# The end of an eight-core encoder kernel: weights of the last group kept resident, its tiles run one after another, early output stores moved

## Chip, cores, metric

One Trainium2 chip, all eight NeuronCores, one program on each. A core computes 2048 of 16384 tokens with a halo of 60 on each side; nothing is exchanged between cores. The metric is the device time of one launch, that of the slowest core, in microseconds (us).

The executions fall into a fast state and a slow one, in which the cores of one die (0 to 3, 4 to 7) or of both show a lower granted TensorE clock. A profile is of one execution; it lists span and granted clock of each core.

## The reference, cut

```python
for l in range(DEPTH):          # 4 layers, D_MODEL 1024, D_FF 2816
    x = layer_norm(ALPHA * x + 0.5 * swiglu_ffn(x, ffn1...), ln1_g, ln1_b)
    x = layer_norm(ALPHA * x + hybrid_mixer(x, ...), ln2_g, ln2_b)
    x = layer_norm(ALPHA * x + 0.5 * swiglu_ffn(x, ffn2...), ln3_g, ln3_b)
# swiglu_ffn: (silu(x @ w_gate) * (x @ w_up)) @ w_down
```

## The kernel before

The activations lie transposed in on-chip memory: 1024 features as 8 chunks of 128 partitions, tokens along the free dimension, as fp32 (`xs`) and as bf16 (`xb`). The tokens of a core are cut into two halves (`s` = 0, 1) and each half into three tiles. While the FFN of one half runs on TensorE, the mixer or the layer norms of the other half run on the other engines. A small list scheduler in Python places every instruction, so each engine executes a fixed order. In the names of the profiles, `bank` is an accumulator of TensorE, `PEld` its weight loads, `sg` and `HF` the gate after silu and the product with up, and `HM`, `Y`, `ringM` memory that belongs to the mixer and is lent to the norms and, in the change, to the weights.

```python
def tiles_of(rng):              # three nearly equal tiles; 352, 352, 352 for the last half
    ...

class Ring:                     # weight blocks of 128 x 1024, five slots, loaded by the POOL queue
    def release(self, k):
        self.load(k + self.ns)  # a freed slot loads the block five places ahead
```

An FFN goes through its 22 blocks of the inner dimension in three groups of 8, 7 and 7. In each group every block is used for all three tiles before the next:

```python
for gi, (j0, nj) in enumerate(GROUPS):      # (0, 8), (8, 7), (15, 7)
    for jj in range(nj):
        kg, ku = ringF.take(), ringF.take()
        for ti, (c0, n) in enumerate(tiles):
            # gate: 8 matmuls, up: 8 matmuls; then silu on ACT, product on DVE -> HF
            ...
        ringF.release(kg); ringF.release(ku)
    for dc in range(NKC):                   # 8 output chunks
        k = ringF.take()
        for ti, (c0, n) in enumerate(tiles):
            # nj matmuls; then xs[dc] += bank on DVE ("evacuation")
            ...
        ringF.release(k)
spawn_ln(s, li, which)                      # three layer norm tiles
```

A layer norm tile sums over the 1024 features with matmuls against ones. VectorE adds pairs of chunks first, so that only four small matmuls are needed. Then come ten VectorE operations for mean and 1/sqrt(var), four "normalise passes" over 4 chunks each, and the affine on ScalarE:

```python
e1 = tt(t1, XS3(0, 2, c0, n), XS3(2, 2, c0, n), ALU.add)   # DVE: pairs of chunks
...                                                        # ACT: squares, DVE: their sums
mm_part(banks[0][1], n, [(ones_v, row_of(t1, c, n)) for c in range(2)], True, True)
pe_ev = mm_part(banks[1][1], n, [(ones_v, row_of(q1, c, n)) for c in range(2)], True, True)
ev = yield from stats(rst, nmr, nm, t_, banks[0], banks[1], n, inv, pr - 0.5)
for h in range(2):
    x = XS3(4 * h, 4, c0, n)
    e1 = tt(x, x, rst, ALU.mult, ...)                      # DVE, 4 x n elements
    zev.append(tt(x, x, nmr, ALU.add, ...))                # DVE, 4 x n elements
...
if final:                                                  # the last norm of the last layer
    dma("sp", dram(out3[:, :, o0:o0 + n]), XS3(0, NKC, c0, n), f"st{s}{ti}", ...)
```

Of the kernel before, what the change touches and what calls it, by code (L numbers as in the profile page):

```python
# [10 lines left out]
ALU = mybir.AluOpType  # L11

P = 128
# [47 lines left out]
def tiles_of(rng):  # L61
    lo, hi = rng
    units = (hi - lo) // 4
    base, rem = divmod(units, 3)
    out = []
    for i in range(3):
        n = 4 * (base + (1 if i < rem else 0))
        out.append((lo, n))
        lo += n
    return out  # L70
# [273 lines left out]
def build():  # L344
# [254 lines left out]
            self.load(k + self.ns)  # L599

    F_ORDER = [(s, li, f) for li in range(nl) for f in range(2) for s in range(2)]
    planF, planM = [], []
    for s, li, f in F_ORDER:
        base = li * 2 + f
        for j0, nj in GROUPS:
            for jj in range(nj):
                row = wgud[base * NJ + j0 + jj]
                planF.append((row[:, 0:1024], 1024))
                planF.append((row[:, 1024:2048], 1024))
            for dc in range(NKC):  # L610
                planF.append((wdd[base * NKC + dc][:, j0 * P:(j0 + nj) * P], nj * P))
# [69 lines left out]
        yield Need("dve", [e1], prio=prio)  # L681
        return tt(nmr, nm, rst, ALU.mult)

    def ln_tile(s, li, which, ti, c0, n, final):
        yp = y_prom(s, li, which)[ti]
        goff, boff = V_LN[which]
        inv = 1.0 / D
        pr = 0.1 * ti
        yield Need("dve", [yp], [(lnp, 1)], prio=pr, cond=lambda: st["m"] == 0)
        st["ln"] += 1  # L690
        u = lnp.get()
        pair = lambda k: lnu_bf(u[1], k, n, 1)
        t1, t2, q1, q2 = pair(0), pair(1), pair(2), pair(3)
        e1 = tt(t1, XS3(0, 2, c0, n), XS3(2, 2, c0, n), ALU.add)
        e2 = None
        for k in range(4):
            yield Need("act", [yp, e2], prio=pr - 0.3)
            e = act(q2 if k else q1, XS3(2 * k, 2, c0, n), AF.Square)
            if k == 0:
                yield Need("dve", [yp], prio=pr - 0.3)  # L700
                tt(t2, XS3(4, 2, c0, n), XS3(6, 2, c0, n), ALU.add)
            else:
                yield Need("dve", [e], prio=pr - 0.3)
                e2 = tt(q1, q1, q2, ALU.add, rate=2.0)
            if k == 1:
                yield Need("dve", [e1], prio=pr - 0.3)
                e1 = tt(t1, t1, t2, ALU.add, rate=2.0)
        yield Need("pe", [e1, e2], [(bankB, 2)], prio=-1e9)
        banks = (bankB.get(), bankB.get())
        mm_part(banks[0][1], n, [(ones_v, row_of(t1, c, n)) for c in range(2)], True, True)  # L710
        pe_ev = mm_part(banks[1][1], n, [(ones_v, row_of(q1, c, n)) for c in range(2)], True, True)
        yield Need("act", [pe_ev], prio=pr - 0.5)
        t_, nm, rst, nmr = [lnu_f32(u[1], k, n) for k in range(4)]
        ev = yield from stats(rst, nmr, nm, t_, banks[0], banks[1], n, inv, pr - 0.5)
        zev = []
        for h in range(2):
            x = XS3(4 * h, 4, c0, n)
            yield Need("dve", [ev], prio=pr)
            e1 = tt(x, x, rst, ALU.mult, bap=bcast(rst, 4, n))
            yield Need("dve", [e1], prio=pr)  # L720
            zev.append(tt(x, x, nmr, ALU.add, bap=bcast(nmr, 4, n)))
        lnp.put(u, zev[1])
        st["ln"] -= 1
        e1 = None
        if not final:
            for c in range(NKC):
                yield Need("act", [zev[c // 4]], prio=pr)
                e1 = act(XB(c, c0, n), XS(c, c0, n), AF.Identity, scale=vcol(goff + c, li), bias=vcol(boff + c, li))
            xb_prom(s, li, which)[ti].add(e1)
        if which == 0 or final:  # L730
            for c in range(NKC):
                yield Need("act", [zev[c // 4]], prio=pr if final else pr + 2)
                if final:
                    act(XS(c, c0, n), XS(c, c0, n), AF.Identity, scale=vcol(goff + c, li), bias=vcol(boff + c, li))
                else:
                    act(XS(c, c0, n), XS(c, c0, n), AF.Identity, scale=agcol(li, c), bias=agcol(li, 8 + c))
        if final:
            o0 = c0 - HALO
            dma("sp", dram(out3[:, :, o0:o0 + n]), XS3(0, NKC, c0, n), f"st{s}{ti}", n * 4 * NKC * P / 1e6)

    def spawn_ln(s, li, which):
        rng = in_range(s, li) if which == 0 else out_range(s, li)
# [13 lines left out]
    def ffn(s, li, f):  # L756
        rng = in_range(s, li) if f == 0 else out_range(s, li)
        tiles = tiles_of(rng)
        lo = rng[0]
        if f == 1:  # L760
            xp, which = xb_prom(s, li, 1), 2
        elif li > 0:
            xp, which = xb_prom(s, li - 1, 2), 0
        else:
            xp, which = x0P[s], 0
        yp = y_prom(s, li, which)
        if f == 0:
            ag = (lambda c: agcol(li - 1, 32 + c)) if li > 0 else (lambda c: ALPHA)
            ab = (lambda c: agcol(li - 1, 40 + c)) if li > 0 else None
        else:  # L770
            ag = lambda c: agcol(li, 16 + c)
            ab = lambda c: agcol(li, 24 + c)
        for gi, (j0, nj) in enumerate(GROUPS):
            slots = [(hs["n"] + i) % NHS for i in range(nj)]
            hs["n"] += nj
            hP = [PromiseN(nj) for _ in range(3)]
            for jj in range(nj):
                kg, ku = ringF.take(), ringF.take()
                for ti, (c0, n) in enumerate(tiles):
                    yield Need("pe", [xp[ti], ringF.ev[kg], ringF.ev[ku]], [(bankF, 2)], prio=f_prio)  # L780
                    g, u = bankF.get(), bankF.get()
                    ge = mm([(g[1], n, [(ringF.w(kg, k), XB(k, c0, n)) for k in range(NKC)])])
                    ue = mm([(u[1], n, [(ringF.w(ku, k), XB(k, c0, n)) for k in range(NKC)])])
                    st["vtF"] += 2 * NKC * n / 2400.0

                    def silu(ti=ti, c0=c0, n=n, g=g, u=u, ge=ge, ue=ue, hslot=slots[jj], hP=hP):
                        b = sgp.get()
                        sg = view2("sg", sg_t, 4, b[1], NMAX, 0, n)
                        ae = act(sg, bank(g[1], n), AF.Silu)
                        bankF.put(g, ae)  # L790

                        def hmul():
                            de = stt(HF(hslot, c0 - lo, n), sg, 0.5, bank(u[1], n), ALU.mult, ALU.mult)
                            bankF.put(u, de)
                            sgp.put(b, de)
                            hP[ti].add(de)
                        S.task(Need("dve", [ae, ue], prio=-1), hmul)
                    S.task(Need("act", [ge], [(sgp, 1)], prio=-1), silu)
                ringF.release(kg)
                ringF.release(ku)  # L800
                if late and gi == 0 and jj > 1:
                    late.pop(0)(ue)
            for dc in range(NKC):
                k = ringF.take()
                for ti, (c0, n) in enumerate(tiles):
                    yield Need("pe", [hP[ti], ringF.ev[k]], [(bankF, 1)], prio=f_prio)
                    b = bankF.get()
                    me = mm([(b[1], n, [(ringF.w(k, i), HF(slots[i], c0 - lo, n)) for i in range(nj)])])
                    st["vtF"] += nj * n / 2400.0

                    def evac(dc=dc, ti=ti, c0=c0, n=n, b=b, gi=gi):
                        x, ps = XS(dc, c0, n), bank(b[1], n)
                        if gi == 0:
                            de = stt(x, x, ag(dc), ps, ALU.mult, ALU.add)
                        elif gi == 1 and ab is not None:
                            de = stt(x, ps, ab(dc), x, ALU.add, ALU.add)
                        else:
                            de = tt(x, x, ps, ALU.add)
                        bankF.put(b, de)
                        if gi == len(GROUPS) - 1:  # L820
                            yp[ti].add(de)
                    S.task(Need("dve", [me], prio=-1), evac)
                ringF.release(k)
        spawn_ln(s, li, which)

    def f_chain():
        for s, li, f in F_ORDER:
# [385 lines left out]
    with ExitStack() as stack:  # L1213
# [22 lines left out]
        def _(e):  # L1236
            p.replay("sp", e, sems)
            for s in range(2):
                for ti in range(3):
                    e.wait_ge(sems[f"st{s}{ti}"], 16)  # L1240
    build.prog = p
    return nc

# [122 lines left out]
```

## Time and profile before

| | kernel before |
|---|---|
| median of all 15 executions, fast and slow | 4927.84 us |
| mean of the 7 fast ones | 4771.3 us |
| profiled execution (fast) | 4776.15 us, cores 4764.0 to 4774.6 |
| TensorE busy | 98% |
| wait of TensorE on a weight load in the last FFN, by core | 4.4 to 11.9 us |
| from the end of the last weight matmul to the end of the span | 57.2 to 60.3 us |

The prediction shows the lines that carry this. Columns: names, issuing queue, count, kB, us from issue to landing.

```profile
out<-xs SPq DMA_DIRECT2D x1, 1408.0 KB, 5.7
```

```profile
out<-xs SPq DMA_DIRECT2D x1, 1408.0 KB, 8.6
```

It is the same last store of the same program. It took 5.6 to 6.2 us on six cores, 8.5 and 8.6 on cores 4 and 5. In the middle of their stores these two moved 200 to 240 GB/s each, the other six some 350 to 380.

### The profile page before, as it was taken

The numbers are of one execution on the slowest core, as the hardware profiler recorded it, in microseconds if no ns is written. First come the engines' busy times: TensorE is split into PE (matmuls) and PEld (weight loads), VectorE is DVE, ScalarE is ACT, GpSimd is POOL, SyncE is SP. The second block draws the span as 40 slices with busy tenths as digits, with TensorE's granted clock in tenths as the row PEclk, the third lists the DMA queues.
The fourth block names the chain that finished last, engine by engine and source line by source line (L and its number), as shares of the span: only waits on it lengthen the run. The fifth ranks groups of instructions, "written<-read, shape, count | busy, mean of one in ns | idle before, by whom it ended". The sixth has DMA issues, their size and how long they took to land.

```text
span 4774.6 us, 80409 instructions; the slowest of 8 cores (4764.0 to 4774.6 us)
## 1 busy us (share of the span) xinstructions
PE 4666.3 (98%) x31440; PEld 3053.1 (64%) x31440; DVE 2760.5 (58%) x4632; ACT 1486.7 (31%) x2751; POOL 808.5 (17%) x1524
## 2 busy tenths in 40 slices
PE   7999999999999999999999999999999999999995
PEld 4666666666666666666666666666666666666563
DVE  2265775762627577566363757757445556756635
ACT  1143343231314334333131433433212242443312
POOL 1112112111111211211111121221111121121110
PEclk9999999999999999999999999999999999999997
DMA  8557558556565755755555665665556575575663
GB/s 146 69 69 107 73 70 110 73 73 73 73 71 72 105 75 80 102 74 73 74 74 74 87 95 74 95 88 75 74 73 77 75 101 85 72 107 72 95 79 67
DMA packets 232106, 394.03 MB, mean 83 GB/s; under 512 B 27456, under 2 KB 85312, under 8 KB 231744
## 3 DMA queue, kind: packets, MB, share of 16 engines
q0 software_dynamic: 204544, 364.77, 59.2%
q1 hardware_dynamic: 27200, 24.12, 2.2%
q8 instruction: 265, 4.34, 0.4%
q14 instruction: 97, 0.79, 0.1%
HBM read 725.32 MB, written 8.39 MB: 154 GB/s over the span
## 4 chain that ended last, share of the span: by engine, by line
PE 93%; DVE 4%; DMA 1%; issue 1%; ACT 1%; SPq 0%; ACTq 0%; POOLq 0%; DVEq 0%
PE bank L492 92%; DVE HM L529 2%; PE bank L500 1%; DVE xs L529 1%; DMA ringF<-wgu 1%; DVE HM L535 1%; DMA xs<-xin 1%; ACT HM L522 0%; DVE HF L535 0%; DVE Y L535 0%; DVE HM L542 0%; ACT xb L522 0%; ACT xs L522 0%; SPq L555 0%; DVE tiny L529 0%
## 5 line engine op out<-in xcount | busy, mean ns | idle before, releaser
L492 PE MATMUL bank<-xb,ringF 128*128 128x352 bf16 (+7 forms) x16896 | 2554.2, 312 | 38.3 <-ACT xb L522 24.8
L492 PEld LDWEIGHTS bank<-xb,ringF 128*128 128x128 bf16 x16896 | 1639.5, 97 | 922.1 <-issue 44.0
L492 PE MATMUL bank<-HF,ringF 128*128 128x352 bf16 (+8 forms) x8448 | 1277.1, 312 | 0.0
L522 ACT ACTIVATE sg<-bank 128x352 f32<-128x352 f32 (+8 forms) x1200 | 555.8, 463 | 2188.3 <-PE bank L492 2170.5
L535 DVE SCALAR_TENSOR_TENSOR HF<-sg,bank 128x352 bf16<-128x352 f32 (+8 forms) x1056 | 547.3, 519 | 1030.0 <-PE bank L492 988.4
L492 PEld LDWEIGHTS bank<-HF,ringF 128*128 128x128 bf16 x8448 | 822.5, 97 | 434.6
L555 POOL DMA_DIRECT2D ringF<-wgu x704 | 371.9, 528 | 2187.0 <-PE bank L492 2148.6
L529 DVE TENSOR_TENSOR xs<-xs,bank 128x352 f32<-128x352 f32 (+8 forms) x624 | 324.1, 521 | 323.0 <-PE bank L492 323.0
L492 PE MATMUL bank<-xb,ringM 128*128 128x352 bf16 (+8 forms) x3264 | 501.0, 313 | 0.2 <-ACT xb L522 0.2
L529 DVE TENSOR_TENSOR xs<-xs,HM 128x1408 f32<-128x1408 f32 (+8 forms) x288 | 464.8, 1617 | 1.2
L529 DVE TENSOR_TENSOR HM<-HM 128x352 f32<-128x352 f32 (+23 forms) x640 | 405.2, 649 | 39.7 <-ACT HM L522 31.2
L492 PEld LDWEIGHTS bank<-xb,ringM 128*128 128x128 bf16 x3264 | 316.8, 97 | 173.6 <-issue 0.9
L522 ACT ACTIVATE HM<-xs 128x704 bf16<-128x704 f32 (+8 forms) x288 | 221.3, 784 | 576.5 <-DVE xs L529 330.5
L555 POOL DMA_DIRECT2D ringF<-wd x384 | 203.5, 530 | 988.1 <-PE bank L492 972.3
L522 ACT ACTIVATE xb<-xs,vecs 128x352 bf16<-128x352 f32 (+7 forms) x528 | 330.3, 673 | 50.0 <-DVE xs L529 49.5
L535 DVE SCALAR_TENSOR_TENSOR xs<-xs,agb,bank 128x352 f32<-128x352 f32 (+3 forms) x336 | 191.7, 578 | 215.3 <-PE bank L492 215.0
L492 PE MATMUL bank<-Y,ringM 128*128 128x352 bf16 (+5 forms) x1584 | 238.5, 311 | 7.1 <-DVE tiny L529 4.4
L535 DVE SCALAR_TENSOR_TENSOR xs<-bank,agb,xs 128x352 f32<-128x352 f32 (+3 forms) x336 | 192.6, 580 | 77.8 <-PE bank L492 77.8
L492 PEld LDWEIGHTS bank<-Y,ringM 128*128 128x128 bf16 x1584 | 154.5, 98 | 88.3 <-issue 9.3
L535 DVE SCALAR_TENSOR_TENSOR HM<-HM 128x352 f32<-128x352 f32 (+12 forms) x320 | 164.9, 515 | 7.2
L535 DVE SCALAR_TENSOR_TENSOR HM<-sg,bank 128x352 bf16<-128x352 f32 (+6 forms) x72 | 125.0, 1737 | 51.0 <-PE bank L492 51.0
L555 POOL DMA_DIRECT2D ringM<-win x136 | 73.3, 540 | 355.1 <-PE bank L492 353.3
(46 smaller groups left out, 1397.0 us busy)
## 6 DMA issues: line engine op xcount, KB each, us to landing
ringF<-wgu POOLq DMA_DIRECT2D x704, 256.0 KB, 5.8
ringF<-wd POOLq DMA_DIRECT2D x256, 224.0 KB, 4.4
ringM<-win POOLq DMA_DIRECT2D x136, 256.0 KB, 4.8
ringF<-wd POOLq DMA_DIRECT2D x128, 256.0 KB, 4.9
ringM<-wcn POOLq DMA_DIRECT2D x96, 288.0 KB, 6.4
ringM<-wout POOLq DMA_DIRECT2D x64, 256.0 KB, 4.5
xs<-xin SPq DMA_DIRECT2D x6, 744.0 KB, 21.2
out<-xs SPq DMA_DIRECT2D x3, 1408.0 KB, 8.6
```

The lines of the kernel that those rows point to most:

```text
L492: ins = e.matmul(banks_t[b][:, :n], l.ap, r.ap, start=(i == 0), stop=(i == len(prs) - 1))
L500: ins = e.matmul(banks_t[b][:, :n], l.ap, r.ap, start=start and i == 0, stop=stop and i == len(prs) - 1)
L522: return p.emit("act", lambda e: e.activation(out=out.ap, in_=in_.ap, func=func, bias=bi, scale=sc), R, [out], dur=k + size_of(out) * 0.00 ...
L529: return dve(lambda e: e.tensor_tensor(out=out.ap, in0=a.ap, in1=bap if bap is not None else b.ap, op=op), out, [a, b], rate)
L535: return dve(lambda e: e.scalar_tensor_tensor(out=out.ap, in0=a.ap, scalar=s_, in1=bap if bap is not None else b.ap, op0=op0, op1=op1), ou ...
L555: return p.emit(eng, lambda e: e.dma_start(out=out.ap, in_=in_.ap), R, W, dur=0.55 if eng == "pool" else 0.6, dma=sem, mbytes=mbytes, afte ...
```

## The change

The intent: two norms of the last FFN shall run under TensorE's work instead of after it, the last tile shall have a short norm, and the stores of the first half shall leave when no weight load is under way. To run tile by tile, all 22 blocks of the last group must be resident; they go into memory that the mixer no longer needs.

```diff
 def tiles_of(rng):
     ...
+        if rng == out_range(1, DEPTH - 1):
+            n = (372, 372, 312)[i]

+    def short_sums(u, yp, c0, n):             # the last tile only
+        for h in range(2):
+            e1 = copy(cast, XS3(4 * h, 4, c0, n))          # DVE: bf16
+            e2 = act(sq, XS3(4 * h, 4, c0, n), AF.Square)  # ACT
+            mm_part(... ones x 4 rows of cast ...); mm_part(... ones x 4 rows of sq ...)

+        if short:                             # affine: six chunks on ACT, two on DVE
+            for h in range(2):
+                ...
+                dma("sp", dram(out3[:, 4 * h:4 * h + 4, o0:o0 + n]), ...)   # store in halves
+            if s == 0:
+                late_st.append(put)           # the first half's stores wait
+            else:
+                put()

+            if (s, li, f, gi) == LAST:
+                spawn_ln(s, li, which)
+                for ti in range(3):
+                    for t, jj in [(ti, j) for j in range(ti > 0, nj)] + [(ti + 1, 0)] * (ti < 2):
+                        ue = yield from gate_up(lastW[2 * jj], lastW[2 * jj + 1], ...)
+                        while late_st:
+                            late_st.pop(0)([ue])
+                    for dc in range(NKC):
+                        yield from down(lastW[2 * nj + dc], ...)
+                return
     ...
+                if (s, li, f) == LAST[:3]:
+                    load_last(1)              # one early block per gate/up step of groups 1, 2
     ...
+                if (s, li, f) == LAST[:3] and gi == 1:
+                    load_last(1)              # and per down chunk of group 2
```

## The prediction

> **What bounds the kernel now.** I began with the page's busy times and its slices: is this one long stage or several?
>
> ```profile
> PE 4666.3 (98%) x31440; PEld 3053.1 (64%) x31440; DVE 2760.5 (58%) x4632; ACT 1486.7 (31%) x2751; POOL 808.5 (17%) x1524
> PE   7999999999999999999999999999999999999995
> PEclk9999999999999999999999999999999999999997
> ```
>
> TensorE is busy for 98% of 4774.6 us. Only the first and last slices (119 us each) have holes. The change doesn't touch the first, and it removes no matmul: what it can win are holes of TensorE. Next, the list of waits from 4300 us until the last large matmul, and the timeline at the place where it points:
>
> ```profile
> PE bank L492 <- DMA ringF<-wgu: 11.9, 1, 11.9
> ```
>
> ```profile
> 4493.07 39.36 SPq L555 DMA_DIRECT2D out<-xs  x3
> ...
> 4502.52 6.13 PE L492 MATMUL bank<-xb,ringF 128*128 128x352 bf16 x40
> 4520.53 14.72 PE L492 MATMUL bank<-xb,ringF 128*128 128x352 bf16 x88 [11.87 <-DMA ringF<-wgu]
> ```
>
> One wait of 11.9 us. It lies inside the three output stores of the first half of the sequence, issued from 4493 us on while the last FFN streams its weights. Reading the same wait on all eight cores, the longest single wait on this load is 7.2, 4.4, 7.9, 9.0, 11.9, 11.9, 8.6 and 6.4 us, against spans of 4770.0, 4764.2, 4766.9, 4769.2, 4774.1, 4774.6, 4764.0 and 4768.7: the slowest two cores are those with the longest stall, so the metric contains nearly all of it.
>
> Then the chain that ended last, in order of time, and the end of the timeline:
>
> ```profile
> 4599.99 113.24 PE bank L492 x759
> 4713.25 0.52 DVE xs L529
> ...
> 4743.03 1.64 DVE xs L529
> ...
> 4761.54 1.64 DVE xs L529
> ```
>
> ```profile
> 4740.77 25.43 SPq L555 DMA_DIRECT2D out<-xs  x3
> ```
>
> TensorE's last weight matmul ends at 4713.2, the span at 4774.6: a tail of 61.4 us in which three layer norms of 352 tokens run one behind another on VectorE. All three start together, because the FFN finishes its three tiles within one microsecond per output chunk. The third norm's sums begin at 4744.6, when VectorE has finished the second's last pass; its last affine on ScalarE ends at 4765.6, and its 1.44 MB store needs another 9.0.
>
> The last view is the busy time by stretch of the last FFN (columns after the times: PEclk, DMA share, GB/s):
>
> ```profile
> 4490.00:4535.00 45.00, 33.13 (x214) 20.96 (x212) 25.61 (x37) 20.43 (x40) 4.62 (x9) 0.89 0.89 127
> 4563.00:4613.00 50.00, 50.00 (x337) 32.35 (x336) 11.32 (x22) 9.46 (x21) 6.86 (x13) 1.00 0.60 72
> 4638.00:4688.00 50.00, 50.00 (x338) 32.34 (x336) 11.60 (x22) 9.31 (x20) 6.87 (x13) 1.00 0.59 73
> ```
>
> A gate/up stretch without stores uses 0.60 of the DMA engines; with the stores it is at 0.89 and TensorE starves.
>
> [...] the records show 0.50 in the tail, so the little sums there cost 0.75 us instead of 0.46 a pair. [...]
>
> **The change, part by part.**
> 1. The last FFN's output tiles become 372, 372, 312 tokens instead of 3 x 352. The sum stays 1056; [...] so TensorE's time is unchanged: 0.
> 2. The last of the FFN's three weight groups (14 gate/up and 8 down blocks) no longer goes through the five-slot ring. Its 22 blocks are loaded early, one after each of 15 gate/up steps and after 7 down steps of groups 1 and 2, into memory of the finished mixer. In gate/up that makes three loads per 7.16 us (48 x 149 ns) instead of two: DMA share 0.60 x 1.5 = 0.90, about 110 GB/s. In the second down stretch the ring's own loads run out, so it is no heavier than now (about 10 loads for 8).
> 3. With all 22 resident, the last group runs tile by tile. Gate+up is 16 matmuls: 2.52 us for 372 tokens, 2.12 for 312. Down is 7 matmuls in 8 chunks: 8.8 and 7.4 us. Call T the end of the last matmul. Tile 0 ends at T - (15.1 + 2.1 + 8.8) - (12.7 + 7.4) = T - 46.2, tile 1 at T - 20.1. So the norms of tiles 0 and 1 move under TensorE.
> 4. The first half's three stores wait for the last group, T - 73, where no weight load is left. 4.1 MB at the some 220 GB/s of the last store (1.44 MB in the 6.5 us that its data moved) take 19 us: done long before tile 0's store. Removed: the stall, 11.9 us on the slowest core.
> 5. The last tile's norm skips the pairwise adds: two casts on VectorE (0.94 us measured for 1488 elements, so 0.8 for 1248), two squares on ScalarE, 16 small matmuls; its store is in halves and VectorE helps with two affines.
>
> The new tail, from T, if VectorE is free: evacuation 0.5; two squares 2 x 1.2 = 2.4 (measured 0.79 for 704 elements, scaled); the second half's matmuls and hand-off 1.4; mean and its square on ScalarE 0.9; ten VectorE statistics operations of 312 elements, 5.2 now for 352 (they start at 4751.6 and end at 4756.8), so 4.8; four normalise passes [...] 1.46 each, 5.8; two affines on ScalarE 1.3; then the half store, 0.64 MB: fixed part 9.0 - 6.5 = 2.5, plus 2.9 of data, plus 1 because the other half is still moving: 6.4. Sum 23.5 us.
>
> VectorE isn't free, though. One norm of 372 costs it 4.0 (sums) + 5.2 (statistics) + 4 x 1.70 = 16.0 us. Between T-46.2 and T-20.1 it must do that plus 7 products and 8 evacuations of 0.54, 24 us in 26. Between T-20.1 and T another 16.0 + 14 x 0.48 = 22.7 us in 20.1. So about 2.6 us of tile 1's norm, and hand-off idle on top, hang over into the tail. Part fits into its hand-offs; I add 1.5. In that crowded stretch TensorE may wait for a product or an evacuation once or twice: I add 1. Tail 26 us instead of 61.4.
>
> Sum: 61.4 - 26 = 35.4, plus 11.9: 47.3 us, 1.0%. The fast timed run of 4769.8 becomes 4722.5; I predict 4723 us for the fast state.
>
> **The rivals.**
> (a) The early loads stall what the stores stalled. For: a share of 0.90 is where TensorE starved. Against: there 127 GB/s moved, with stores of 1.33 MB before the load in need; here the third load is issued last, so the next period's first one meets at most its end. A load needs 4.4 to 6.9 us to land and has some 8.35 (7.16 + 1.2 from release to the end of the step). Also, in mixer stretches (1580 to 1600 us: share 0.89, 120 GB/s) TensorE was busy for 20.00 of 20 us. If it were wrong: 0.5 us in each of 15 steps, 4730.
> (b) VectorE becomes the bound of the last 46 us. 24 + 22.7 us before T and about 14 for the last norm make 60.7 us, which can't end before T+14.5; the serial chain puts VectorE's last work near T+17. So it is close, not ahead. If VectorE's fixed order keeps tile 1's normalise passes ahead of tile 2's chain and delays products on TensorE, 6 to 10 us come back: about 4731.
> (c) The stall isn't the stores' doing, or they stall the last group instead. Then only 35 us: 4735. Against: the stall's size orders the cores, and no weights are loaded any more in the last group.
> (d) Better than thought: tile 1's norm ends before T and the halves overlap fully: tail 21, 4717.
>
> **Range and chances.** Adding (a) and (b) gives 4739; (c) with (b) about 4744. (d) gives 4717[...]. So 4705 to 4748. A gain of 2% would be 95 us: stall and whole tail together are 73 us, so this can't happen by the mechanism. Slower by 2% would need a stall in each of the changed steps of 6 us or more. Faster by over 2%: 0.01; within 2%: 0.98; slower: 0.01.
>
> **What would show it.** In the changed profile: no wait of several microseconds on a ring load after 4490 us; cores closer together than now (10.6 us); DMA share near 0.9 in the first two gate/up stretches with TensorE full; three stores at the start of the last group; last weight matmul near 4702 us (4713.2 - 11.9 + 1), with two norms before it; tail near 26 us, of which about 6 are the last half store. It is wrong if a new wait stands before the early loads, if TensorE has gaps above 3 us in the last 46 us before T, or if the tail stays above 35.

The tail after is 23.5 + 1.5 + 1 = 26 us, and the gain 61.4 - 26 + 11.9 = 47.3 us. These measured times lead to the same estimates:

- Matmuls: 149 ns for 352 columns is 50.00 us over 336 in the stretch from 4563 us. Scaled by the width, 16 matmuls take 2.52 us for 372 columns and 2.11 for 312. The changed kernel then measured 157.5 ns for 372 (104 in 16.38 us from 4628.78, core 2) and 132.5 for 312, so one matmul on each of the three tiles takes 447.5 ns, against 446.4 before.
- Normalise passes: the trace of the kernel before has 521 ns for a TENSOR_TENSOR on fp32 of 352 elements and 1703 for one of 1488. The line through the two gives 1.45 us for 1248 (the prediction has 1.46), and the changed kernel measured 1453 ns.
- The half clock: 0.50 in the tail of core 5 from 4721 us on, read from the trace. Why a store slows a weight load of another queue was not shown, nor, before run 6, what a store in halves gains; that the stores made the wait of 4.4 to 11.9 us, runs 1 and 2 show.
- The range: its ends lie 12 us under the lowest rival (4717) and 4 above the highest (4744).

## The result

| | before | after |
|---|---|---|
| median of all executions, fast and slow | 4927.84 (15) | 4890.56 (12) |
| mean of the fast executions | 4771.3 (7) | 4730.5 (4) |
| profiled execution | 4776.15 | 4731.14 |
| cores in the profile | 4764.0 to 4774.6 | 4722.2 to 4729.6 |

The ratio is 0.9915, with a 95% interval of 0.9901 to 0.9929: within 2%, 40.7 us. Ratios are the mean time of one kernel's fast runs over that of the other's fast runs of the same rounds, so not quite the ratio of the medians in the table. The medians are those of slow executions: 8 of the 12 were slow.

The busy times and slices of the changed kernel, to set beside the first fence of the prediction:

```profile
PE 4668.8 (99%) x31452; PEld 3056.1 (65%) x31452; DVE 2756.5 (58%) x4630; ACT 1481.1 (31%) x2747; POOL 808.4 (17%) x1524
PE   7999999999999999999999999999999999999998
PEclk9999999999999999999999999999999999999999
```

TensorE is busy for as long as before (4668.8 against 4666.3 us), but the last slice has gone from 5 tenths to 8: the span lost idle time, not work. Next, the waits of TensorE from 4300 us to the end (core 2, the slowest):

```profile
PE bank L494 <- DVE HF L537: 2.5, 1, 2.5
PE bank L502 <- DVE ringM L548: 1.4, 1, 1.4
PE bank L502 <- ACT HM L524: 0.2, 1, 0.2
```

The wait on a weight load is gone, on this and on every other core. A new one of 2.5 us has come, on a VectorE product, also on every core. The second and third lie in the tail. The timeline where the new wait stands (columns: start, us, engine, instruction, idle time before it and its releaser):

```profile
4698.22 1.70 DVE L531 TENSOR_TENSOR xs<-xs,HM 128x1488 f32<-128x1488 f32 x1
4699.84 0.47 DVE L537 SCALAR_TENSOR_TENSOR HF<-sg,bank 128x312 bf16<-128x312 f32 x1
...
4700.46 9.23 PE L494 MATMUL bank<-HF,Y 128*128 128x312 bf16 x56 [2.49 <-DVE HF L537]
```

The third tile's last product stands behind a normalise pass of the second tile's norm in VectorE's fixed order, and TensorE waits for it. The third line has something more: 56 matmuls of 312 columns should take 7.4 us (132.5 ns each, as the 40 from 4691.45 to 4696.75 us took), and took 9.23; on core 4 they took 7.58. The busy time by stretch tells why. It gives the same 3.3 us after the wait on core 2 and on core 4 (columns: stretch, length, busy us and count of PE, PEld, DVE, ACT, POOL, then granted clock, DMA share, GB/s):

```profile
4700.46:4703.76 3.30, 3.30 (x13) 1.93 (x14) 2.75 (x3) 1.80 (x4) 0.00 (x0) 0.50 0.02 5
```

```profile
4694.45:4697.75 3.30, 3.30 (x25) 2.43 (x26) 3.30 (x3) 1.79 (x4) 0.00 (x0) 1.00 0.02 5
```

On core 2 the granted clock is 0.50 and 13 matmuls run; on core 4, after the same wait, it is 1.00 and 25 run. Six of the eight cores fell to half clock there, and each lost 1.65 us more.

The same view for the stages of the last FFN (core 2): first gate/up with early loads, second down with early loads, start of the last group with the first half's stores, second tile of the last group:

```profile
4466.00:4516.00 50.00, 50.00 (x337) 32.54 (x335) 45.91 (x78) 27.41 (x52) 10.02 (x19) 1.00 0.68 100
...
4603.70:4628.70 25.00, 25.00 (x170) 16.23 (x168) 13.95 (x24) 0.00 (x0) 6.54 (x13) 1.00 0.78 120
4628.80:4657.70 28.90, 28.90 (x186) 17.92 (x184) 8.67 (x16) 4.66 (x9) 0.00 (x0) 1.00 0.82 142
4657.80:4684.40 26.60, 26.60 (x173) 16.70 (x172) 22.26 (x35) 12.19 (x21) 0.00 (x0) 1.00 0.00 1
```

TensorE is full in all of them. The share of the DMA engines with three loads per step is 0.68, for 100 GB/s: not the 0.90 of the prediction. In the last line VectorE is busy for 22.26 of 26.60 us: the first tile's norm runs under TensorE's matmuls.

Finally the end of the chain that ended last:

```profile
4698.22 1.70 DVE xs L531
4699.92 0.40 DVE HF L537
4700.32 0.14 issue
4700.46 5.53 PE bank L494 x28
...
4719.06 1.38 DVE xs L531
...
4723.32 1.47 DVE xs L531
4724.79 0.02 issue
4724.81 0.65 ACT xs L524
```

One norm is left after the last weight matmul (4709.7 us), where there were three.

To compare the two kernels I cut every core's span at two points of its timeline: the start of the last FFN and the end of its last weight matmul. Means over the eight cores of the profiled executions:

| us | start of last FFN | last FFN | of it: waits on loads | tail | span |
|---|---|---|---|---|---|
| before | 4461.9 | 248.9 | 8.4 | 58.2 | 4769.0 |
| after | 4462.4 | 243.3 | 0 | 20.1 | 4725.8 |
| gain | -0.5 | 5.6 | | 38.1 | 43.2 |

This table is the measure in what follows, since the start of the last FFN differs from core to core and run to run (4457 to 4466 us) and hides effects of a few microseconds in the total time.

### The profile page after: what moved, and what is told of

The parts are those of the page before. It is cut to its first block, busy times and chain, and to the rows that moved or that the text cites. A ratio compares the mean times of both kernels' runs of the same rounds, so it can differ in the third digit from the quotient of the medians.

```text
span 4729.6 us, 80377 instructions; the slowest of 8 cores (4722.2 to 4729.6 us)
## 1 busy us (share of the span) xinstructions
PE 4668.8 (99%) x31452; PEld 3056.1 (65%) x31452; DVE 2756.5 (58%) x4630; ACT 1481.1 (31%) x2747; POOL 808.4 (17%) x1524
## 3 DMA queue, kind: packets, MB, share of 16 engines
q0 software_dynamic: 204544, 364.77, 53.3%
## 4 chain that ended last, share of the span: by engine, by line
PE 95%; DVE 3%; DMA 1%; issue 1%; ACT 1%; SPq 0%; ACTq 0%; DVEq 0%; POOLq 0%
PE bank L494 94%; DVE HM L531 1%; PE bank L502 1%; DVE xs L531 1%; DMA xs<-xin 1%; DVE HM L537 0%; ACT HM L524 0%; DVE HF L537 0%; DMA ringF<-wgu 0%; DVE Y L537 0%; DVE HM L544 0%; ACT xb L524 0%; ACT xs L524 0%; SPq L557 0%; ACT sg L524 0%
## 5 line engine op out<-in xcount | busy, mean ns | idle before, releaser
L494 PE MATMUL bank<-xb,ringF 128*128 128x352 bf16 (+9 forms) x16560 | 2503.6, 312 | 27.1 <-ACT xb L524 24.7
L494 PE MATMUL bank<-HF,ringF 128*128 128x352 bf16 (+9 forms) x8280 | 1251.8, 312 | 0.0
L524 ACT ACTIVATE sg<-bank 128x352 f32<-128x352 f32 (+9 forms) x1200 | 553.9, 462 | 2185.2 <-PE bank L494 2163.0
L537 DVE SCALAR_TENSOR_TENSOR HF<-sg,bank 128x352 bf16<-128x352 f32 (+9 forms) x1056 | 545.9, 517 | 997.2 <-PE bank L494 964.9
L531 DVE TENSOR_TENSOR xs<-xs,bank 128x352 f32<-128x352 f32 (+9 forms) x624 | 323.2, 520 | 318.5 <-PE bank L494 318.3
L531 DVE TENSOR_TENSOR xs<-xs,HM 128x1408 f32<-128x1408 f32 (+9 forms) x288 | 464.1, 1614 | 1.1
L531 DVE TENSOR_TENSOR HM<-HM 128x704 bf16<-128x704 bf16 (+16 forms) x636 | 403.0, 649 | 39.3 <-ACT HM L524 30.8
L524 ACT ACTIVATE HM<-xs 128x704 bf16<-128x704 f32 (+10 forms) x286 | 220.8, 787 | 551.2 <-DVE xs L531 323.2
L524 ACT ACTIVATE xb<-xs,vecs 128x352 bf16<-128x352 f32 (+8 forms) x528 | 328.9, 670 | 49.4 <-DVE xs L531 49.0
L494 PE MATMUL bank<-Y,ringM 128*128 128x352 bf16 (+6 forms) x1584 | 238.6, 311 | 7.1 <-DVE tiny L531 4.4
```

Of the source, the lines that this page charges most:

```text
L494: ins = e.matmul(banks_t[b][:, :n], l.ap, r.ap, start=(i == 0), stop=(i == len(prs) - 1))
L524: return p.emit("act", lambda e: e.activation(out=out.ap, in_=in_.ap, func=func, bias=bi, scale=sc), R, [out], dur=k + size_of(out) * 0.00 ...
L531: return dve(lambda e: e.tensor_tensor(out=out.ap, in0=a.ap, in1=bap if bap is not None else b.ap, op=op), out, [a, b], rate)
L537: return dve(lambda e: e.scalar_tensor_tensor(out=out.ap, in0=a.ap, scalar=s_, in1=bap if bap is not None else b.ap, op0=op0, op1=op1), ou ...
```

## The experiments

Eleven kernels ran, all correct. Their means over eight cores, as above; the ratio is against the kernel before, in rounds of their own:

| run | last FFN | tail | fast time (runs) | ratio |
|---|---|---|---|---|
| before | 248.9 | 58.2 | 4771.3 (7) | 1 |
| after | 243.3 | 20.1 | 4730.5 (4) | 0.9915 |
| 1 before, late stores | 239.5 | 57.3 | 4765.5 (5) | 0.999 |
| 2 after, stores at once | 250.1 | 20.3 | 4739.4 (5) | 0.9935 |
| 3 after, old order | 238.1 | 56.4 | 4767.3 (1) | none |
| 4 after, old sums | 243.3 | 21.8 | 4730.1 (3) | 0.9943 |
| 5 after, equal tiles | 241.0 | 22.1 | 4727.4 (4) | 0.9911 |
| 6 after, one store | 242.7 | 23.4 | 4731.8 (4) | 0.992 |
| 7 after, passes held | 240.4 | 24.2 | 4730.5 (4) | 0.9918 |
| 8 after, denser loads | 246.2 | 20.3 | 4731.7 (4) | 0.992 |
| 9 after, wait filled | 242.1 | 20.2 | 4727.4 (3) | 0.99 |
| 10 equal tiles, held prefetch | 241.0 | 22.2 | 4721.8 (5) | 0.9888 |
| 11 equal tiles, prefetch held less | 241.0 | 21.9 | 4730.1 (1) | 0.9955 |

Two rows leave out runs that the record counts as fast: in run 4 one of 4783.58 us, in run 11 four of 4756.68 to 4765.2, in each of which some cores had a clock of 0.984 to 0.991 where the others had 0.995 or more. The ratios contain them, so they have wide intervals (0.9874 to 1.0013 and 0.9913 to 0.9996). Two of the six fast runs of the kernel before that belong to runs 9 to 11 are of this kind too (4798.77 and 4799.18), so these three ratios flatter: against the mean of the other four they would be 0.9913, 0.9901 and 0.9918.

The runs came in three groups of rounds, each on another chip. The kernel before took 4770.8 us in the group of runs 1 to 4, 4769.7 in that of 5 to 8 and 4769.1 (those four) in that of 9 to 11, against the 4771.3 that stand beside the changed kernel. A difference of some 2 us between times of different groups therefore shows nothing by itself.

### 1. The kernel before with late stores only

```diff
+                if (s, li, f, gi) == F_ORDER[-1] + (2,) and dc == 2:
+                    while late_st:
+                        late_st.pop(0)([me])
```

> The kernel before, with one thing changed: the three output stores of the first half of the sequence wait until the last weight block has been issued to the ring (third down chunk of the last group). If the stores made the stall (my theory): no wait of TensorE on a weight load after 4460 us on any core (before: 4.4 to 11.9 us), the last weight matmul 8 us earlier on average, the tail still 57 to 60 us, fast time 8 to 10 us below before (ratio 0.998). Rival, the stall has another cause: the wait of 4 to 12 us stays and the ratio is 1.000. Second rival, the moved stores delay the stores of the tail: the wait is gone but the tail grows by 3 us or more and the time gains less than 5 us.

Measured: no wait on a load on four cores, 0.8 to 4.0 us on the others; the last FFN 9.4 us shorter on average, the tail 57.3. This shows that the stores made the stall. The gain of the last FFN is larger than the wait of 8.4 us itself, and where it is free of stalls the FFN takes 238.14 us: before, 10.8 us were lost, 8.4 waiting and some 2.4 at half clock after it. (The clock in the 3.4 us after core 5's wait of 11.9 us was 0.57; over all eight cores, read in steps of 1 us, the lowered clock after the wait cost 1.5 to 2.9 us, 2.25 on average.) In time only 5 us came of it, less than expected and not clear of the noise (0.9974 to 1.0006): the slowest core counts, in this kernel the last ring loads are still under way when the stores start, and core 7, the slowest of the profile, waited 4.0 us for a down block. In the changed kernel, with resident weights, no such wait is left.

### 2. The changed kernel with the stores at once

```diff
-            if s == 0:
-                late_st.append(put)
-            else:
-                put()
+            put()
```

> The changed kernel, but the three stores of the first half leave as soon as their norm is done, as in the kernel before. If stores and weight loads collide: a wait on a weight load comes back between 4490 and 4540 us, and because three loads per step are under way instead of two it is larger than before, 10 to 20 us; fast time 4740 to 4750 (ratio to before 0.994). Rival, the early loads don't add to it: 8 us as before, 4738. Rival, the stall isn't the stores' doing: no wait, 4730.

Measured: waits of 2.3 to 6.9 us on all cores, in one to three pieces; the last FFN 6.8 us longer, the time 8.9 us longer. Two lines of core 0, the slowest:

```profile
PE bank L494 <- DMA ringF<-wgu: 3.8, 1, 3.8
PE bank L494 <- DMA ringF<-wd: 3.1, 1, 3.1
```

The collision is back, so both runs agree on its cause. That the early loads make it larger than before is not borne out: 4.9 us of waiting on average against 8.4. Core 0 lost 10.1 us in all, 3.2 more than it waited: the clock was 0.50 for some us after each of the two.

### 3. The changed kernel with the last group in the old order

```diff
-                for ti in range(3):
-                    for t, jj in [(ti, j) for j in range(ti > 0, nj)] + [(ti + 1, 0)] * (ti < 2):
+                for jj in range(nj):
+                    for t in range(3):
...
-                    for dc in range(NKC):
+                for dc in range(NKC):
+                    for t in range(3):
```

> The changed kernel (early loads, late stores, short last norm, 372/372/312) with the last weight group run in the old order, all three tiles per block. If running tile by tile is what shortens the tail: three norms stand after the last weight matmul again, VectorE work there 16 + 16 + 14 = 46 us and a half store of 4, tail near 50 us instead of 20; the last weight matmul comes 4 us earlier than in the changed kernel (no wait of 2.5 us on a product, no sums of two norms of 0.65 us each between the matmuls); fast time 4756 (ratio 0.997). Rival, the short last norm and the stores are the larger part: tail under 35 us, time under 4743.

Measured: a tail of 52.4 to 55.1 us on six cores, and a last FFN of 238.1 us on all eight. Running tile by tile is what shortens the tail, by 33 us (53.3 on these six cores, 20.1 in the changed kernel), and it costs 5.2 us inside the last FFN: the wait of 2.5, the half clock of 1.65 on six of eight cores, and 1.3 us for two sets of small matmuls against ones (0.63 us for the first, in the chain), which used to run in the tail on an idle TensorE. On cores 2 and 3 the tail was 65.6 us: their last two stores took 26.1 us (1488 kB) and 16.4 us (624 kB) to land, 12.3 and 3.4 on core 4. These two cores ended their matmuls 0.26 us apart; cores 0 and 1, though, ended theirs 0.19 us apart and had tails of 54.4 and 55.1 us, so closeness alone doesn't explain it. The slow stores are why the one fast run took 4767.3 us and not 4756; the mean span of the other six cores was 4751.4.

### 4. The changed kernel with the old sums in the last tile

```diff
-        if short:
-            banks, pe_ev = yield from short_sums(u, yp, c0, n)
-        else:
-            banks, pe_ev = yield from sums(pr, yp, t1, t2, q1, q2, c0, n)
+        banks, pe_ev = yield from sums(pr, yp, t1, t2, q1, q2, c0, n)
```

> The changed kernel with the old way of summing in the last tile's norm (pairwise adds on VectorE, four squares), the store still in halves. If the short sums lie on the path: the time from the last evacuation to the first statistics operation grows from 4.0 us to about 6.5 (the old sums took 7.0 us for 352 elements in the kernel before), fast time 4733 (ratio 0.992). Rival, VectorE still works off the second tile's norm at that time and the old sums hide behind it: no change, 4730.5. Rival, the old sums compete with that rest and cost more: 5 us or more, 4736.

Measured: tail 21.8 us instead of 20.1, so the short sums are worth 1.7 us, less than expected. In the time it can't be seen: the three undisturbed fast runs (4730.1) are no slower.

### 5. Equal tiles

```diff
-            n = (372, 372, 312)[i]
+            n = 352
```

> The changed kernel with 352/352/352 tokens instead of 372/372/312. If the small last tile pays: the last tile's chain grows with its size, four normalise passes by 0.17 us each, ten statistics operations by 0.04 each, sums and squares by 0.3, half store by 0.35, together the tail 20.0 -> 21.8 us; fast time 4732. Rival, the smaller second tile (15.1 us of VectorE work instead of 16.0, and 22.7 us of TensorE work to hide it instead of 20.1) takes away the wait of TensorE for a product (2.5 us and the half clock after it, 1.65 us) and more than makes up: 4728.

Measured: 4727.4 us, 3.1 below the changed kernel, but the kernel before was 1.6 lower in these rounds too, and the ratios can't be told apart (0.9911 against 0.9915, intervals of 0.0014 on each side or more). The stages show more. Both theories are right at once: the tail grew by 2.0 us, and the last FFN shrank by 2.3, since the wait for the product is 1.5 us instead of 2.5 and the clock did not fall on any core (241.02 us on all eight). So the small last tile, a part of the change, gains nothing that these runs can show.

### 6. One store and eight affines on ScalarE for the last tile

```diff
-        if short:
+        if False:      # the branch with halves
...
-        if final and not short:
+        if final:
```

> The changed kernel with the last tile's store in one piece and its eight affines on ScalarE. If the split store lies on the path: two affines more on ScalarE behind the last pass cost 1.1 us, and 1.25 MB land 2.2 us later than the last half (3.4 us), the tail grows from 20.0 to 23.3 us, fast time 4733.8. Rival, the halves compete and the single store is as fast: tail 21, 4731.5.

Measured: tail 23.4 us, +3.3, as expected. The time grew by 1.3 us only, between two groups of rounds. In this run's profile the clock fell on three cores instead of six, which may be the reason; whether it did so in the timed executions too, no record shows.

### 7. The second tile's passes held back

```diff
+            if final and s == 1 and ti == 1:
+                yield Need("dve", [ev], prio=pr, cond=lambda: hlast[0].t is not None)
```

(`hlast` holds the third tile's products; the passes are placed when the last of them has been.)

> The changed kernel, but the second tile's four normalise passes on VectorE are placed behind the last product of the third tile. If the pass of 1.70 us in front of that product makes TensorE wait 2.5 us, and the wait makes the clock fall to half for some 3.3 us (loss 1.65 us on six of eight cores): the wait falls to 0.8 us, the clock stays at 1.00, the last weight matmul comes 3.4 us earlier, the tail grows by 0.4 us since one pass now lies ahead of the casts; fast time 4727.5. Rival, the gain comes back in full because the passes push out the third tile's norm: tail 23, 4730.5.

Measured: the wait is 0.9 us, the FFN 240.43 us on all eight cores, 2.9 less than the changed kernel's mean; but the tail is 24.2 us, 4.1 longer. The rival won: nothing is left of the gain. The timeline of core 2 shows where it went:

```profile
4701.96 0.48 DVE L531 TENSOR_TENSOR xs<-xs,bank 128x312 f32<-128x312 f32 x1 [0.18 <-PE bank L494]
4702.35 1.70 DVE L531 TENSOR_TENSOR xs<-xs,HM 128x1488 f32<-128x1488 f32 x1
4703.97 1.52 DVE L548 CAST ringM<-xs 128x1248 bf16<-128x1248 f32 x2
...
4704.92 0.69 PE L502 MATMUL bank<-ringM,ones 128*128 128x312 bf16 x4 [3.00 <-DVE ringM L548]
4706.06 1.20 PE L502 MATMUL bank<-HM,ones 128*128 128x312 bf16 x4 [0.45 <-ACT HM L524]
```

The fourth pass now stands between the last evacuation and the casts; the small matmuls wait 3.0 us instead of 1.4, the clock falls there (on all eight cores, about 1 us after the wait, where it stayed at 1.00 in the changed kernel), and sets of them take 1.20 us instead of 0.69. Core 2 is not typical in one thing: on cores 2 and 3 the tail was 25.6 and 26.2 us, with half stores of 5.7 and 6.4 us (median of the two), where the other six had 23.4 to 23.9 and 3.5 to 3.7.

### 8. Denser early loads

```diff
-                    load_last(1)
+                    load_last(2)
```

> The changed kernel with two early blocks instead of one after each gate/up step, so four loads per 7.16 us instead of three, in the first ten steps. If the busy share of the DMA engines is what limits (prediction: 0.60 for two loads, 0.90 for three): 1.2 for four, a backlog of 1.4 us per step, waits of TensorE on weight loads of 8 us or more, 4739. Rival, the share isn't proportional to the loads (three loads gave 0.67 in the changed kernel): share 0.75 to 0.85, no wait, 4730.5.

Measured: 116 GB/s at a share of 0.87 in the first 50 us, and no wait on any load. But the last FFN is 2.9 us longer. The timeline tells that it isn't the loads:

```profile
4502.87 0.70 PE L502 MATMUL bank<-HM,ones 128*128 128x328 bf16 x2 [2.53 <-DVE HM L531]
```

TensorE waits 2.5 us for the sums of a norm of the first half, and the clock is 0.50 in the 3.3 us after that (0.97 over the first 50 us). The scheduler, which models the loads, has put ScalarE's and VectorE's instructions in another order there. The loads themselves don't limit at four per step; the rival is right on that, and neither theory had foreseen the new wait.

### 9. The wait filled with matmuls

```diff
+                    if ti == 2:
+                        b = bankF.get()
+                        bankF.put(b, mm([(b[1], n, [(lastW[0][0](k % NKC), XB(k % NKC, c0, n))
+                                                    for k in range(12)])]))
```

> The changed kernel with twelve matmuls of 312 columns into a spare bank (their result is thrown away) in front of the third tile's down part, where TensorE waits 2.5 us for the last product. If that wait lets the clock fall to half for some 3.3 us afterwards: TensorE is now idle for only 0.9 us there, the clock stays at 1.00 on all eight cores, and the last FFN takes 242.05 us on all of them instead of 243.7 on six and 242.05 on two; fast time 4729. Rival, the half clock there has another cause: it stays, 243.7 us on most cores, 4730.5.

Measured: 242.05 us (242.04 to 242.05) on all eight cores, where the changed kernel has 243.7 on six; fast time 4727.4, 3.1 lower, of which 2.2 are also the difference of the kernel before between the two groups of rounds. The clock in the 3.3 us after the wait, core 2:

```profile
4697.73:4701.03 3.30, 3.30 (x25) 2.42 (x26) 3.30 (x3) 1.80 (x4) 0.00 (x0) 1.00 0.00 0
```

25 matmuls instead of 13. This shows that the half clock came of the idle wait. Twelve useless matmuls in the gap make the last FFN shorter; in the time of the kernel these runs can't show it.

### 10. Equal tiles, and the prefetch at the start held until the second tile's input is there

```diff
-    ringF.start(2, NSF)
+    for m in range(2, NSF):
+        ringF.load(m, [x_ev[3]])     # second half of the second tile's input has landed
```

> The best version so far (equal tiles) with the lesson of the stores used at the kernel's start: the prefetch of ring slots 3 to 5 (1.5 MB read) waits until the input of the second tile has landed, instead of competing with the inputs. If competition delays the first inputs: the first matmul at 12.5 us instead of 18, the second wait for an input (6.8 us) no longer, the last FFN starts 5 us earlier (4456.5 us on average), fast time 4722.5. Rival, the bytes as a whole are the limit: TensorE waits for weight blocks instead, start of the last FFN and time unchanged, 4727.4.

Measured: 4721.8 us, 5.6 below the equal tiles alone (5.0 below, if the 0.6 us are taken off by which the kernel before was faster in these rounds). The last FFN starts at 4454.3 us on average instead of 4461.6. The way there differs from the expectation: the first matmul comes at 16.9 us, hardly earlier, but the waits after it shrink to 0.8 and 1.8 us (core 3):

```profile
16.93 5.00 PE L494 MATMUL bank<-xb,ringF 128*128 128x372 bf16 x16 [16.93 <-ACT xb L524]
22.74 2.68 PE L494 MATMUL bank<-xb,ringF 128*128 128x372 bf16 x16 [0.81 <-ACT xb L524]
27.23 33.08 PE L494 MATMUL bank<-xb,ringF 128*128 128x372 bf16 x209 [1.81 <-ACT xb L524]
```

In the kernel before, the second input was awaited for 6.8 us. This is the fastest version, faster than both kernels.

### 11. The same, held until the first tile's input only

```diff
-        ringF.load(m, [x_ev[3]])
+        ringF.load(m, [x_ev[1]])
```

> As the run with the held prefetch, but the prefetch waits only for the first tile's input. If competition delays the first inputs: first matmul at 12.5 us too, but the wait for the second tile's input stays at 6 us or more, gain 3 us, 4724.5. Rival, no gain: 4727.4.

Measured: no gain in the one undisturbed run. The waits for inputs sum to 28.2 us on the slowest core against 24.8 before, and the last FFN starts at 4463.0 us. The slowest core, 1:

```profile
17.30 4.21 PE L494 MATMUL bank<-xb,ringF 128*128 128x372 bf16 x16 [17.30 <-ACT xb L524]
22.67 2.68 PE L494 MATMUL bank<-xb,ringF 128*128 128x372 bf16 x16 [1.17 <-ACT xb L524]
35.05 25.24 PE L494 MATMUL bank<-xb,ringF 128*128 128x372 bf16 x141 [9.69 <-ACT xb L524]
```

The expectation missed the place. The wait for the second tile's input did not stay at 6 us, it fell to 2.3 us or less; the third tile's input came late instead, with a wait of 6.7 to 10.4 us on all eight cores (at most 1.8 in the kernel before). That the prefetch then meets the third tile's input is my reading; the transfers themselves were not looked at.

## Why the prediction was right and wrong

**The range failed.** The recorded median of all executions, 4890.56 us, lies far above "So 4705 to 4748". The step that failed is "Range and chances": the only scatter it allowed for was a small figure. Within the fast state the scatter measured was small indeed: the 7 fast executions of the kernel before lay within 0.07% (4769.21 to 4772.51 us), the 4 of the changed kernel within 0.03% (4729.76 to 4731.14). But of the three times of the kernel before that were known then, two were of the slow state (4927.84 and 5583.97), and of the twelve executions of the changed kernel eight were (4808.88 to 5543.15). A range that leaves the slow state out says nothing of such a median. The prediction's 4723 us answers only for the fast state, as it says; there 4730.5 was measured, inside the range, and the ratio of the fast runs was within 2%, as it gave with 0.98.

**Within the fast state the mechanism was right, and terms of the sum were mis-sized.** The gain was 40.7 us, not 47.3. The first such step is "The fast timed run of 4769.8 becomes 4722.5". The terms 61.4 and 11.9 were read on core 5 of the profiled execution, which took 4776.15 us, and taken off another execution that was 6.3 us shorter. In the profiled one, cores 4 and 5 happened to run 0.4 us apart, had the two longest stalls, and a last store of 8.5 us where the other six had 5.6 to 6.2. Subtracting 47.3 from its own 4776.15 would have given 4728.9. The slowest core of one execution isn't the typical one, and the prediction took it for that, though it listed the stalls of the other seven. Nor does "the stall's size orders the cores" hold in that list: below the first two, core 6 with 8.6 us had the shortest span of all, and core 0 with 7.2 the third longest. When the longest stall goes, another core becomes the slowest.

**Term by term:**
- Stall, 11.9 us: the mechanism is right (runs 1 and 2). Its size was 8.4 us on average, plus 2.4 of half clock after it that the prediction left out, although it had read a clock of 0.50 in the tail: 10.8.
- Tail before, 61.4: it was 58.2 on average, 60.3 on core 5. Of the difference, 1.0 us is a reading error: the chain goes through the second tile's evacuation at 4713.25, but the third tile's matmuls ended at 4714.3.
- Tail after, 25 us without the wait of TensorE: measured 20.1. Most of its terms hold. From the timeline, statistics took 4.8 us (predicted 4.8), the passes 5.8 (5.8), the two affines 1.2 (1.3). The half store was mis-sized: 6.4 predicted from core 5's slow store, 3.6 measured from the end of the last affine. The rest of the second tile's norm, predicted at 1.5 us of VectorE, isn't in the tail: its passes stand between the evacuations of the third tile, and on core 2 the last of them ended at 4708.1 us, before the last weight matmul (4709.7). What is left is one of its affines on ScalarE, 0.59 us between the two squares in the chain.
- "In that crowded stretch TensorE may wait ... I add 1": 2.5 us of wait and 1.65 of half clock on six of eight cores (run 9), and 1.3 us for the norms' small matmuls, which the prediction did not count (part 1 says "TensorE's time is unchanged", part 3 has only gate/up and down): 5.2 us in all rather than 1. Here the path itself was wrong and not only a number: the prediction let TensorE pass over the two hidden norms nearly free of cost.

From 4722.5 to 4730.5, in means: +1.5 for the base (4771.3 instead of 4769.8), +1.1 for the stall (10.8 instead of 11.9), +3.2 for the tail before, +4.2 for the new waits, -4.9 for the tail after, +0.5 for the start of the last FFN: 5.6 of 8.0 us. The other 2.4 lie in what means don't hold: the time is the slowest of eight cores, and which core that is changed from execution to execution (core 2, 6, 5 and 0 in the four fast ones of the changed kernel). I have not itemised them.

**The rivals.** (a) The early loads stalling: wrong, as predicted, though not for the given reason. Three loads per step had a share of 0.68, not 0.60 x 1.5 = 0.90; four had 0.87 without a wait on a load. The share isn't proportional to the bytes: 73 GB/s went with 0.59 and 100 with 0.68, and 142 with 0.82, less than the 0.87 of 116 (run 8). (b) VectorE as the bound of the last 46 us: mostly right. It was "close, not ahead", and what (b) feared is what came: a normalise pass of tile 1 ahead of tile 2's product. It cost 2.5 us and up to 1.65 of half clock, not 6 to 10, and relieving it (run 7) gave all of it back in the tail. That (b)'s 4731 is near the measured 4730.5 is luck, since other terms were off by more. (c) The stall not the stores' doing: ruled out by runs 1 and 2. (d) A tail of 21: that is what came, 20.1, but not its 4717, since the tail before was over-read and the waits of TensorE under-read.

**Signs named beforehand:** no ring wait, cores closer (7.4 instead of 10.6 us), full gate/up stretches, three stores at the start of the last group, two norms under the matmuls, no gap above 3 us: all seen. The share of 0.9 and the tail of 26 were not; the last matmul was at 4705.7 us on average, not 4702.

## What to carry to other kernels

Take the terms of a prediction from the execution whose time they are subtracted from, and look at all cores before calling the slowest one typical; and say for which state of the chip a time is predicted. A wait of TensorE costs more than its length if the clock falls after it: filling a gap of 2.5 us with useless matmuls was worth 1.65 us of the last FFN on the six cores where it had fallen. When two norms are hidden under matmuls, count what the hiding engine must do in that time: where VectorE was busy for 21.0 of the third tile's 25.3 us (core 2), a fixed order that puts one long pass in front of one short product stopped TensorE, and moving the pass only moved the loss. Transfers with slack should not start beside transfers that are awaited: for the stores this gave 9.4 us of the last FFN (5 us of the time, run 1), for the prefetch at the start 7.3 us up to the start of the last FFN (5.6 us of the time, run 10).

## Measured here, and left open

- An idle gap of TensorE of 2.5 us was enough on six of eight cores in the same program: clock 0.50 for the next 3.3 us, 1.65 us lost. A gap of 1.5 us (run 5) or 0.9 us (runs 7 and 9) there was not. In run 2 a gap of 2.3 us on core 5 was enough too; one of 1.9 us on core 6 in run 1 was not. Why two cores kept the full clock after the gap of 2.5 us, no run shows.
- Why some of the last stores are slow stays open. A last store of 1408 kB landed in 8.5 and 8.6 us on two neighbours that ended 0.4 us apart (each counted from the start of its own span), and in 5.6 to 6.2 us on the cores whose neighbour was 2.49 us or more away; in run 3 one of 624 kB took 16.4 us against 3.4. But other neighbours as close showed little (0.19 us in run 3, half stores of 5.4 and 6.2 us) or nothing (0.38 us in run 5). No run here tried a cause.
- Stores beside a stream of weight loads: three stores of together 4 MB made TensorE wait 4.4 to 11.9 us.
